# Two-layer diffusion backbone: attention maxima in other PSUM banks, five weight units in flight, later row sums, an output gate ahead of the heads

## The chip, the cores and the metric

The kernel runs on one core of one Trainium2 chip. The metric is the device time of one execution in microseconds (us), as the median of several runs. Everything below about durations and waits is read from one profiled execution of the kernel before the change.

## The reference, cut to what matters

Two layers work on 512 latent tokens (x) and 256 context tokens (ctx), 1024 channels, in float32. Each layer normalises, projects the tokens into three mixers, merges these by sigmoid gates, and ends with a gated MLP:

```python
for l in range(DEPTH):
    hx = rmsnorm(x, norm1_w[l]) * (1.0 + sc1) + sh1          # context likewise
    mix_x, mix_c = token_mixers(hx, hc, ...)
    x = x + g1 * mix_x
    x = x + g2 * conv_ffn(rmsnorm(x, norm2_w[l]) * (1.0 + sc2) + sh2, ...)
    # the context takes the same steps in layer 0 only
def token_mixers(hx, hc, ...):
    conv_x = conformer_conv(...)                             # depthwise, width 31
    h_x, h_c = mlstm_bidirectional(...)                      # 4 heads of 256, both directions
    mlstm_x = mlstm_readout(h_x, mo_x, ...)                  # rms norm, sigmoid(mo_x) as output gate
    attn_x = latent_attention(q_x, [k_c, k_x], [v_c, v_x])   # 8 heads of 64, 768 keys
    return (g_conv * conv_x + g_mlstm * mlstm_x + g_attn * attn_x) @ w_out
def attend(q, k, v):
    p = jax.nn.softmax(einsum(q, k) * 64 ** -0.5)            # each query's maximum is subtracted
```

## The kernel before, in words

Every float32 product is three products of rounded parts: a high part (`hh`, `B`, `AC`; `wh` for weights) and a low part (the remainder: `hl`, `C`; `wl`). A projection (`proj`, matmuls at L717) takes one 128x128 weight block at a time and multiplies it with the stretch of 512 latent and of 256 context columns into an `mm` tile in PSUM; a matmul over 512 columns issues every 0.23 us, one over 256 every 0.12 us.

**Weights.** A unit is four blocks (256 KB). Its DMA is queued on SP (`raw`), ScalarE (ACT) copies it to the high part `wh` (L215), and GpSimd (POOL) forms the low part `wl` (L217). The three tags have three buffers each, and units are split two ahead (`SPLITS`). In stretches with `shared` set, odd units are loaded into `P` tiles, and VectorE (DVE) forms their low part. These are the stretches in which matmuls have only 256 columns: the merge of the context in the first layer (1136 to 1165 us) and the start of its up projection, the context's part of the last down projection (1764 to 1790), and the second layer's merge (2597 to 2657) with the start of its up projection.

**PSUM.** Two `pv` tiles and two `sm` tiles of 512 columns; `mm` has two tiles of 1024 columns in the first layer and four of 512 in the second (`banks`). Projections use `mm`; `pv` takes the accumulator of the attention's value product (L1565), the maxima's scores (L1472, L1479) and the maxima's transposes (L1489).

**Order.** Each engine runs its instructions in the order in which the program is written; `Filler` sets that order. `step()` issues one piece of projection work on TensorE (PE), and `tick()` counts down the side chains (`chain`), which say with `yield n` after how many ticks their next piece is issued. Ticks set only the order: an instruction then waits for its inputs, and everything behind it on the same engine waits too.

**Gates.** `mgates` turns the mLSTM gate rows into decay terms: a chain of small DVE operations (L852 to L893) with two ACT operations between, and at its end four PE matmuls (`sm<-t,cst`, L904).

**mLSTM heads.** Tables `HEADS` and `HEADS1` (second layer) give, per head, the projections that fill it (`c` convolution taps, `o0 o1` output gates, `q`, `v` of the next head) and the tick of each step. `S` multiplies three pairs of scores, `score_gap` ticks apart, and sums them into `den` (DVE, L1131); `R` (`normalise`) sums `den` over rows by PE (L584), sends the result through a DMA and applies it (DVE, L1157); `V` multiplies with the values. Indices 0 and 1 are the two column groups.

**Attention.** `prepare(i)` needs, per head, each query's maximum before `weigh` can exponentiate: four maxima of 512 latent keys (`mx`), then two of twice 256 context keys (`mc`), one `pv` tile and one DVE reduction each, `prep` ticks apart; then `rp`, a transpose of the maxima (L1489, L1490). In the first layer a pair of context queries follows. While head i+1 is prepared, `weigh` and L1565 finish head i: reciprocal (L1571) and scaling out of `pv` (L1573).

Of the kernel before, what the change touches and what calls it, by code (L numbers as in the profile page):

```python
# [10 lines left out]
F32R = mybir.dt.float32r  # L11
# [6 lines left out]
D = 1024  # L18
# [32 lines left out]
HEADS = [["c o0 o1 q v", "0:D1 2:S0 6:R0 9:S1 18:D2 22:V0 24:R1 26:S2 41:R2 44:V1 60:V2 60:D*"]] * 3 +     [["c o0 o1 b b x0", "0:D1 2:S0 6:R0 9:S1 18:D2 24:R1 26:S2 28:V0 40:R2 44:V1 52:s 56:V2"]]  # L51
HEADS1 = [["c o0 o1 q v", "2:S0 4:D1 16:R0 22:S1 39:R1 40:V0 61:V1 61:D*"]] * 3 +     [["c o0 o1 b b x0", "2:S0 4:D1 15:R0 21:S1 35:R1 38:V0 51:V1 51:s"]]
COMMON = dict(
    
    gates=[(branch, m) for branch in (1, 0, 2) for m in range(KC)],
    score_gap=5, rows_gap=4, mask_gap=2, prep=2)
OPT = [dict(COMMON, partial=2, heads=HEADS, early=1, first_max=5, send_gap=2, norm_gap=8, first="G v",
            fgroups=[4, 4, 4, 4, 2, 4], skew=2,
            exp2=(0, 1, 2, 3, 4, 5), lo_pool=(0, 1, 2, 5),
            ylo="p", add="d", dve_lo=(0, 2, 4, 6)),  # L60
       dict(COMMON, partial=3, heads=HEADS1, early=1, first_max=8, send_gap=3, norm_gap=11, first="Q g K v",
            fgroups=[4, 3, 4, 4, 3, 4], skew=1,
# [125 lines left out]
class Weights:  # L188


    def __init__(self, nc, dram, l, pool, more):
        self.next, self.shared, self.more = None, False, more
# [14 lines left out]
    def split(self, upto):  # L207
        if self.next and upto > self.units:
            self.next.split(upto - self.units)
        for u in range(len(self.parts), min(upto, self.units)):  # L210
            self.load(u + 1)
            raw = self.raws.pop(u)
            hi = self.pool.tile([128, UNIT * 128], F32R, tag="wh", name=f"wh{self.l}_{u}")
            lo = self.pool.tile([128, UNIT * 128], F32R, tag="wl", name=f"wl{self.l}_{u}")
            self.nc.scalar.activation(out=hi, in_=raw, func=AF.Copy)  # L215
            eng = self.nc.vector if self.shared and u % 2 else self.nc.gpsimd
            eng.tensor_tensor(out=lo, in0=raw, in1=hi.bitcast(F32), op=ALU.subtract)  # L217
            self.parts[u] = hi, lo

    def take(self, *specs):  # L220

        u, j = divmod(len(self.blocks), UNIT)
        if j == 0:
            self.split(u + 1)
        if j <= 1 < j + len(specs):
            self.split(u + SPLITS + 1)
        if j + len(specs) == UNIT:
            self.load(u + LOADS + 1 + 3 * self.shared)
        self.blocks += specs
        o = slice(j * 128, (j + len(specs)) * 128)  # L230
        return [part[:, o] for part in self.parts[u]]
# [56 lines left out]
def build(tc, A):  # L288
# [3 lines left out]
    with ExitStack() as es:  # L292
# [462 lines left out]
        more = lambda u: alloc("P", PB, UNIT * 128)  # L755
        W = Weights(nc, A["ws"], 0, wp, more)
        first = ada_first()
# [19 lines left out]
        for l in range(DEPTH):  # L777
# [10 lines left out]
            if wc:  # L788
                W.next = Weights(nc, A["ws"], l + 1, wp, more)
            plans.append(W.blocks)  # L790
# [35 lines left out]
            def mgates(gp):  # L826
# [16 lines left out]
                for P_, nat, sc in dirs:  # L843
# [12 lines left out]
                yield 1  # L856
                act.activation(out=ln[R, :], in_=u[R, :], func=AF.Ln)
                act.activation(out=u[R, :], in_=ln[R, :], func=AF.Exp, scale=-1.0)
                dve.tensor_tensor(out=e[R, :], in0=e[R, :], in1=u[R, :], op=ALU.mult)
                yield 2  # L860
                dve.tensor_tensor(out=ln[R, :], in0=ln[R, :], in1=e[R, :], op=ALU.subtract)
                yield 1
# [3 lines left out]
                yield 2  # L866
                dve.tensor_tensor_scan(out=ms[R, :], data0=lf[R, :], data1=li[R, :], initial=NEG, op0=ALU.add, op1=ALU.max)
                yield 2
                dve.tensor_tensor_scan(out=g[R, :], data0=rm[R, :], data1=lf[R, :], initial=0.0, op0=ALU.mult, op1=ALU.add)
                yield 2  # L870
                rr, em, be = z, e, u
                for P_, nat, sc in dirs:
                    dve.tensor_tensor(out=rr[P_, nat], in0=g[P_, sc], in1=ms[P_, sc], op=ALU.subtract)
                act.dma_start(out=rdram, in_=rr[R, :])
                yield 1
                for P_, nat, sc in dirs:
# [4 lines left out]
                for d in range(1, NB):  # L881
# [3 lines left out]
                    else:  # L885
# [4 lines left out]
                                  in1=selrow[R].rearrange("p (n o) -> p n o", o=1).to_broadcast([36, 8, 15]), op=ALU.mult)  # L890
                yield 3
# [3 lines left out]
                yield 2  # L895

# [408 lines left out]
            for what in opt["first"].split():  # L1305
# [147 lines left out]
            def prepare(i):  # L1453
# [13 lines left out]
                for o, n, s in own:  # L1467
                    q0, nb = o // 128, n // 128
                    if s == 0:
                        for qb in range(q0, q0 + nb):  # L1470
                            ps = pv()
                            pe.matmul(ps, q1[:, qb * 128:qb * 128 + 128], ks_[v_][:, 0:L], start=True, stop=True)  # L1472
                            dve.reduce_max(out=mx[:, qb:qb + 1], in_=ps, axis=AX.X)
                            yield opt["prep"]
                    m_ = mc if s == 0 else mx
                    for qb in range(q0, q0 + nb, 2):
                        ps = pv()
                        for j in range(2):
                            pe.matmul(ps[:, j * C:j * C + C], q1[:, (qb + j) * 128:(qb + j) * 128 + 128], ks_[v_][:, L:T],  # L1479
                                      start=(j == 0), stop=True, skip_group_check=True)  # L1480
                        dve.reduce_max(out=m_[:, qb:qb + 2], in_=ps.rearrange("p (j n) -> p j n", j=2), axis=AX.X)
                        if qb + 2 < q0 + nb:
                            yield opt["prep"]
                    if s == 0:
# [286 lines left out]
```

## Time and profile before

| | |
|---|---|
| median of 3 runs | 3040.97 us (3040.7 to 3048.51) |
| profiled execution, own time | 3040.4 us |
| its span in the trace | 3038.6 us |
| mean granted TensorE clock | 0.973 of full speed |
| PE busy | 2827.8 us, 93% of the span |
| DVE, ACT, POOL busy | 60%, 38%, 38% |

The span lies 1.8 us below the execution's own time. Idle time counts only on an engine that others wait for; here that is PE.

### The profile page before, as it was taken

Reading aid. Unit: us, or ns where it says so; the run is one execution under the profiler, and the core shown is the slowest. Engines: PE = TensorE matmul, PEld = TensorE weight load, DVE = VectorE, ACT = ScalarE, POOL = GpSimd, SP = SyncE. Lnnn points to the kernel's source line nnn. Section 1 sums busy time; section 2 is a strip of 40 time slices with the busy share of each in tenths; the row PEclk is TensorE's granted clock in tenths of the full one; section 3 lists DMA queues with packets and bytes.
Section 4 is the critical chain, followed back from the end, with each engine's and each line's share of the span. In section 5 each row is a group of like instructions: output and inputs, shape, how many; then the busy total and the mean of one; then the engine's idle time right before and its main releaser. Section 6 shows DMA issues by size and latency. Waiting matters only on the chain. (4 is left out here: it accounts for less than half of the span.)

```text
span 3038.6 us, 42068 instructions
## 1 busy us (share of the span) xinstructions
PE 2827.8 (93%) x15970; PEld 2381.7 (78%) x15970; DVE 1817.7 (60%) x2521; ACT 1156.8 (38%) x2122; POOL 1146.6 (38%) x931
## 2 busy tenths in 40 slices
PE   7999999899889998999999988999889889899999
PEld 4888888787667887888888867887767567778887
DVE  4376787825554336876765555777774763554444
ACT  5224334324345334322322253433444344443333
POOL 2233343224244334333333333333344345444444
PEclk9999999999999999999999999999999999999999
DMA  6454334221010242333333232333322112423333
GB/s 242 133 149 69 58 67 68 49 60 52 28 28 29 63 130 93 115 101 118 118 115 115 75 102 68 65 75 67 65 75 69 39 38 76 154 87 100 93 96 110
DMA packets 156681, 262.47 MB, mean 86 GB/s; under 512 B 17784, under 2 KB 37624, under 8 KB 156480
## 3 DMA queue, kind: packets, MB, share of 16 engines
q1 hardware_dynamic: 142560, 249.67, 28.0%
q10 hardware_dynamic: 13920, 10.12, 3.1%
q8 instruction: 126, 2.06, 0.3%
q14 instruction: 75, 0.61, 0.1%
HBM read 247.05 MB, written 5.46 MB: 83 GB/s over the span
## 5 line engine op out<-in xcount | busy, mean ns | idle before, releaser
L217 POOL TENSOR_TENSOR wl<-raw,wh 128x512 fp32r<-128x512 f32 x659 | 904.6, 1379 | 1507.6 <-ACT wh L215 1461.0
L717 PE MATMUL mm<-hh,wh 128*128 128x512 f32 (+1 forms) x2672 | 963.6, 361 | 17.0 <-DVE big L1619 7.1
L717 PE MATMUL mm<-hh,wl 128*128 128x512 f32 (+1 forms) x2672 | 949.1, 355 | 10.7 <-POOL wl L217 10.6
L717 PE MATMUL mm<-hl,wh 128*128 128x512 f32 (+1 forms) x2672 | 954.4, 357 | 2.1 <-POOL hl L372 1.2
L215 ACT ACTIVATE wh<-raw 128x512 fp32r<-128x512 f32 x662 | 411.2, 625 | 580.2 <-PE mm L717 358.4
L717 PEld LDWEIGHTS mm<-hh,wh 128*128 128x128 f32 x2672 | 512.4, 192 | 113.3 <-issue 29.6
L717 PEld LDWEIGHTS mm<-hh,wl 128*128 128x128 f32 x2672 | 510.4, 191 | 89.4 <-POOL wl L217 15.5
L717 PEld LDWEIGHTS mm<-hl,wh 128*128 128x128 f32 x2672 | 512.3, 192 | 71.4 <-POOL hl L372 1.8
L717 PE MATMUL mm<-C,wh 128*128 128x512 f32 (+1 forms) x1168 | 410.2, 351 | 0.3 <-DVE C L372 0.3
L717 PE MATMUL mm<-B,wh 128*128 128x512 f32 (+1 forms) x976 | 344.4, 353 | 24.4 <-DVE big L1619 11.8
L717 PE MATMUL mm<-B,wl 128*128 128x512 f32 (+1 forms) x976 | 342.5, 351 | 9.2 <-POOL wl L217 8.8
L993 DVE SCALAR_TENSOR_TENSOR AC<-G,par,AC 128x783 f32<-128x783 f32 (+1 forms) x240 | 261.1, 1088 | 3.6
L717 PEld LDWEIGHTS mm<-C,wh 128*128 128x128 f32 x1168 | 226.6, 194 | 28.3 <-DVE C L372 0.5
L717 PEld LDWEIGHTS mm<-B,wh 128*128 128x128 f32 x976 | 190.1, 195 | 53.7 <-ACT wh L215 14.5
L717 PEld LDWEIGHTS mm<-B,wl 128*128 128x128 f32 x976 | 189.4, 194 | 37.4 <-POOL wl L217 14.2
L1669 DVE SCALAR_TENSOR_TENSOR AC<-mm,par,AC 128x511 f32<-128x511 f32 (+1 forms) x132 | 86.7, 656 | 199.0 <-ACT AC L1667 199.0
L1619 DVE SCALAR_TENSOR_TENSOR big<-mm,mod,big 128x512 f32<-128x512 f32 (+1 forms) x144 | 91.1, 657 | 116.3 <-PE mm L717 116.1
L1667 ACT ACTIVATE AC<-mm,par 128x768 f32<-128x768 f32 (+1 forms) x88 | 77.4, 880 | 145.0 <-PE mm L717 144.8
L372 POOL TENSOR_TENSOR P<-t,P 128x512 fp32r<-128x512 f32 (+1 forms) x64 | 75.1, 1175 | 139.2 <-ACT t L1550 111.2
L527 DVE SCALAR_TENSOR_TENSOR P<-C,cs,P 128x512 f32<-128x512 f32 x112 | 116.5, 1072 | 0.9 <-DMA C<-aw 0.9
L1565 PE MATMUL pv<-P,B 128*128 128x512 f32 (+1 forms) x336 | 94.6, 387 | 12.1 <-DVE G L1573 5.2
L1097 ACT ACTIVATE C<-rb,bias 128x128 f32<-128x128 f32 x312 | 96.4, 390 | 21.4 <-DMA rb<-rows 11.2
(282 smaller groups left out, 3726.5 us busy)
## 6 DMA issues: line engine op xcount, KB each, us to landing
raw<-ws SPq DMA_DIRECT2D x662, 256.0 KB, 2.6
C<-aw SPq DMA_DIRECT2D x104, 256.0 KB, 3.0
big<-aw SPq DMA_DIRECT2D x64, 256.0 KB, 4.7
P<-ws SPq DMA_DIRECT2D x30, 256.0 KB, 2.9
big<-xt SPq DMA_DIRECT2D x16, 384.0 KB, 6.3
rb<-rows ACTq DMA_DIRECT2D x40, 128.0 KB, 4.2
den<-rd ACTq DMA_DIRECT2D x40, 64.0 KB, 6.3
den<-rd SPq DMA_DIRECT2D x40, 64.0 KB, 6.3
```

Of the source, the lines that this page charges most:

```text
L215: self.nc.scalar.activation(out=hi, in_=raw, func=AF.Copy)
L217: eng.tensor_tensor(out=lo, in0=raw, in1=hi.bitcast(F32), op=ALU.subtract)
L372: (eng or dve).tensor_tensor(out=out, in0=src, in1=hi.bitcast(F32), op=ALU.subtract)
L527: dve.scalar_tensor_tensor(out=a_, in0=r_, scalar=cs[:, k, q:q + 1], in1=a_, op0=ALU.mult, op1=ALU.add)
L717: pe.matmul(ps[:, o:o + n], w[w_], h[h_][:, so:so + n], start=(k == 0 and i == 0 and o % 512 == 0), stop=(k == n_k - 1 and i == 2), skip_g ...
L993: dve.scalar_tensor_tensor(out=a, in0=t[:, j:j + cw], scalar=par(l, "cw", w0 + j), in1=a, op0=ALU.mult, op1=ALU.add)
L1097: act.activation(out=t[:, off + x * 128:off + x * 128 + 128], in_=rb[:, c0:c0 + 128], func=AF.Exp, bias=bcol(dr, h, key, qb))
L1565: pe.matmul(o_[:, 0:n_q], vblock(b, a_)[:, 64 * v_:64 * v_ + 128], b_[:, 0:n_q], start=(ki == 0 and x == 0), stop=(last and x == 2))
L1619: dve.scalar_tensor_tensor(out=xs[m][:, o:o + n], in0=ps[:, po:po + n], scalar=gain[:, m, s:s + 1], in1=xs[m][:, o:o + n], op0=ALU.mult, o ...
L1667: act.activation(out=t[:, 0:tq], in_=ps[:, 0:tq], func=AF.Identity, scale=fw(1), bias=fb)
L1669: dve.scalar_tensor_tensor(out=t[:, o + 1:o + n], in0=ps[:, o:o + n - 1], scalar=fw(0), in1=t[:, o + 1:o + n], op0=ALU.mult, op1=ALU.add)
```

## The change

Four edits. (A) The maxima over the head's own keys are written to `mm` tiles, as many query blocks to a tile as fit (`banks[1] // L`): in the first layer two latent maxima of 1024 columns and one context maximum of 1024 for a head; in the second layer the counts stay and only the bank changes. The context's own queries stay in `pv`. (B) In `shared` stretches odd units put both parts into the four `AC` tiles (`room`), so that five units can be split instead of three, and splits run one unit further ahead. (C) In the second layer `score_gap` is 4 instead of 5, the first row sums stand at tick 18 instead of 16 and the second at 41 instead of 39 in heads 0 to 2, with the second scores at 25 instead of 22; head 0 loses `o0`. (D) `mgates` yields 33 ticks instead of 21 in all, in both layers, and the second layer issues the first output gate (`o`) before `v`.

```diff
-HEADS1 = [["c o0 o1 q v", "2:S0 4:D1 16:R0 22:S1 39:R1 40:V0 61:V1 61:D*"]] * 3 + ...
+HEADS1 = [["c o1 q v", "2:S0 4:D1 18:R0 25:S1 41:R1 42:V0 60:V1 60:D*"]] + [["c o0 o1 q v", "2:S0 4:D1 18:R0 25:S1 41:R1 42:V0 61:V1 61:D*"]] * 2 + ...
-       dict(COMMON, partial=3, heads=HEADS1, early=1, first_max=8, send_gap=3, norm_gap=11, first="Q g K v",
+       dict(COMMON, partial=3, score_gap=4, heads=HEADS1, early=1, first_max=8, send_gap=3, norm_gap=11, first="Q g K o v",
...
-            hi = self.pool.tile([128, UNIT * 128], F32R, tag="wh", name=f"wh{self.l}_{u}")
-            lo = self.pool.tile([128, UNIT * 128], F32R, tag="wl", name=f"wl{self.l}_{u}")
+            if self.shared and u % 2:
+                hi, lo = self.room(), self.room()
+            else:
+                hi = self.pool.tile([128, UNIT * 128], F32R, tag="wh", name=f"wh{self.l}_{u}")
+                lo = self.pool.tile([128, UNIT * 128], F32R, tag="wl", name=f"wl{self.l}_{u}")
...
-            self.split(u + SPLITS + 1)
+            self.split(u + SPLITS + 1 + self.shared)
...
+        room = lambda: tac(UNIT * 128, F32R)
...
-                yield 5
+                yield 6
                 dve.tensor_scalar(out=u[R, :], in0=e[R, :], scalar1=1.0, scalar2=None, op0=ALU.add)
...
+                elif what == "o":
+                    fill.add(o_gate(0, 0))
...
+                    for to, keys_, per in ((mx, slice(0, L), banks[1] // L), (mc, slice(L, T), banks[1] // C)):
+                        if s:
+                            to, per = mx, 2
+                        if s and keys_.start == 0:
+                            continue
+                        nk = keys_.stop - keys_.start
+                        for qb in range(q0, q0 + nb, per):
+                            ps = mm(per * nk) if s == 0 else pv()
+                            for j in range(per):
+                                pe.matmul(ps[:, j * nk:j * nk + nk], q1[:, (qb + j) * 128:(qb + j) * 128 + 128],
+                                          ks_[v_][:, keys_], start=(j * nk % 512 == 0), stop=True, skip_group_check=True)
+                            dve.reduce_max(out=to[:, qb:qb + per], in_=ps[:, 0:per * nk].rearrange("p (j n) -> p j n", j=per),
+                                           axis=AX.X)
+                            if keys_.start == 0 or qb + per < q0 + nb:
+                                yield opt["prep"]
```

What this moves on DVE is seen in one head of the first layer's attention. Before, from the last two latent maxima on:

```order
L1473 TENSOR_REDUCE mx_7898<-pv_7989 128x1
L1481 TENSOR_REDUCE mc_7899<-pv_8004 128x2
L1481 TENSOR_REDUCE mc_7899<-pv_8017 128x2
L1485 TENSOR_TENSOR mx_7898<-mx_7898,mc_7899 128x4
L369 SCALAR_TENSOR_TENSOR t_807_8039<-sig_7952,mm_7972 128x768
L1446 TENSOR_TENSOR big_6097<-big_6097,t_807_8039 128x768
L1571 RECIPROCAL den_8045<-den_8045 128x256
L1573 TENSOR_TENSOR G_7002<-pv_7910,den_8045 64x256 x2
L1490 SCALAR_TENSOR_TENSOR C_7893<-pv_8051,cst 4x512
L1481 TENSOR_REDUCE mx_7898<-pv_8070 128x2
L1490 SCALAR_TENSOR_TENSOR C_7893<-pv_8097,cst 2x256
```

In the changed kernel, from the second maximum on (line numbers are some nine higher; the maxima over own keys now come from `mm`):

```order
L1489 TENSOR_REDUCE mx_7874<-mm_7931 128x2
L376 TENSOR_TENSOR P_7942<-t_781_7944,P_7941 128x512
L1489 TENSOR_REDUCE mc_7875<-mm_7947 128x4
L1494 TENSOR_TENSOR mx_7874<-mx_7874,mc_7875 128x4
L1499 SCALAR_TENSOR_TENSOR C_7869<-pv_7974,cst 4x512
L1489 TENSOR_REDUCE mx_7874<-pv_7992 128x2
L373 SCALAR_TENSOR_TENSOR t_794_8016<-sig_7929,mm_7954 128x768
L1454 TENSOR_TENSOR big_6097<-big_6097,t_794_8016 128x768
L1499 SCALAR_TENSOR_TENSOR C_7869<-pv_8019,cst 2x256
L1580 RECIPROCAL den_8025<-den_8025 128x256
L1582 TENSOR_TENSOR G_7004<-pv_7886,den_8025 64x256 x2
```

The reciprocal and the scaling of the head before (`RECIPROCAL`, `G`) stood ahead of the transposed maxima (`C`) and of the context's maximum (`128x2`); now these stand ahead of the reciprocal.

On PE the maxima now take the `mm` tile that the open projection leaves free. One place of the changed kernel in the first layer; `mm_7675` is the projection that has just begun, `mm_7682` and `mm_7698` are maxima:

```order
L721 MATMUL mm_7675<-AC_6852,wl_134_7531 128x256
L1487 MATMUL mm_7682<-B_6845,C_7638 128x512 x2
L1574 MATMUL pv_7652<-P_7632,B_6796 128x512
L1574 MATMUL pv_7652<-P_7633,B_6796 128x512
L1574 MATMUL pv_7652<-P_7632,B_6797 128x512
L1553 MATMUL sm_7689<-C_7053,B_6845 128x512
L1554 MATMUL sm_7689<-C_7054,B_6847 128x512
L1487 MATMUL mm_7698<-B_6845,C_7638 128x512 x2
L721 MATMUL mm_7675<-AC_6928,wh_134_7530 128x512
L721 MATMUL mm_7675<-C_6929,wh_134_7530 128x512
```

The tile of `mm_7682` is that of the projection that ended just before `mm_7675`, and `mm_7698` takes the tile of `mm_7682`; before, both were in `pv`.

On DVE the gate chain of the second layer stood nearly in one piece before (`L372` is a low part of a key projection):

```order
L861 TENSOR_TENSOR C_16188<-C_16188,C_16186 36x768
L372 TENSOR_TENSOR B_16273<-mm_16204,B_16272 128x512
L372 TENSOR_TENSOR B_16273<-mm_16205,B_16272 128x256
L864 SCALAR_TENSOR_TENSOR C_16189<-C_16185,C_16188 32x512
L864 SCALAR_TENSOR_TENSOR C_16189<-C_16185,C_16188 32x256
L864 SCALAR_TENSOR_TENSOR C_16189<-C_16185,C_16188 4x512
L864 SCALAR_TENSOR_TENSOR C_16189<-C_16185,C_16188 4x256
L867 SCALAR_TENSOR_TENSOR C_16190<-C_16189,C_16184 36x768
L869 SCALAR_TENSOR_TENSOR C_16191<-sig_16200,C_16189 36x768
```

In the changed kernel the low parts of both key projections stand within it:

```order
L376 TENSOR_TENSOR B_16224<-mm_16156,B_16223 128x512
L376 TENSOR_TENSOR B_16224<-mm_16157,B_16223 128x256
L866 TENSOR_TENSOR C_16140<-C_16140,C_16138 36x768
L869 SCALAR_TENSOR_TENSOR C_16141<-C_16137,C_16140 32x512
L869 SCALAR_TENSOR_TENSOR C_16141<-C_16137,C_16140 32x256
L869 SCALAR_TENSOR_TENSOR C_16141<-C_16137,C_16140 4x512
L869 SCALAR_TENSOR_TENSOR C_16141<-C_16137,C_16140 4x256
L872 SCALAR_TENSOR_TENSOR C_16142<-C_16141,C_16136 36x768
L376 TENSOR_TENSOR B_16298<-mm_16229,B_16297 128x512
L376 TENSOR_TENSOR B_16298<-mm_16230,B_16297 128x256
L874 SCALAR_TENSOR_TENSOR C_16143<-sig_16152,C_16141 36x768
```

The chain's operations are the same; one projection's low part (two operations) that came after it now stands ahead of its second scan (`C<-sig,C`).

## Rows read from the trace of the kernel before

**Rows 1.** The page, part 1: busy us, share of the span, instructions.

```profile
PE 2827.8 (93%) x15970; PEld 2381.7 (78%) x15970; DVE 1817.7 (60%) x2521; ACT 1156.8 (38%) x2122; POOL 1146.6 (38%) x931
```

**Rows 2.** Waits of PE, whole span: total us, times, longest us.

```profile
PE sm L584 <- DVE den L1131: 31.8, 13, 4.0
PE pv L1472 <- DVE mx L1473: 24.0, 19, 6.6
PE mm L717 <- POOL wl L217: 20.2, 27, 2.6
...
PE sm L904 <- DVE t L889: 11.7, 2, 8.6
```

**Rows 3.** Eight half-clock stretches: one window (PEclk behind POOL), and the sum, busy us.

```profile
2061.60:2068.40 6.80, 5.99 (x20) 4.23 (x21) 5.88 (x10) 0.00 (x0) 0.25 (x1) 0.50 0.22 42
...
sum 30.70, PE 29.89 PEld 25.30 DVE 23.07 ACT 6.95 POOL 6.34; mean PE 3.74 PEld 3.16 DVE 2.88 ACT 0.87 POOL 0.79
```

**Rows 4.** Waits of PE, first-layer attention: 740 to 815, then 815 to 960.

```profile
PE pv L1472 <- DVE mx L1473: 7.1, 3, 6.6
...
PE pv L1565 <- DVE G L1573: 4.4, 2, 2.2
PE pv L1479 <- DVE G L1573: 4.2, 2, 2.3
PE pv L1565 <- DVE B L1573: 2.2, 1, 2.2
...
PE pv L1479 <- DVE B L1573: 1.9, 1, 1.9
```

**Rows 5.** Groups on DVE 735 to 1000, and one on ACT 815 to 960.

```profile
L1473 DVE TENSOR_REDUCE mx<-pv 128x1 f32<-128x512 f32 x32 | 21.8, 685 | 8.5 <-PE pv L1472 8.4
...
L1047 DVE TENSOR_TENSOR t<-G,rb 32x512 f32<-32x512 f32 x4 | 6.2, 1555 | 0.1
...
L1573 DVE TENSOR_TENSOR G<-pv,den 64x256 f32<-64x256 f32 x8 | 3.4, 422 | 0.5
...
L1573 DVE TENSOR_TENSOR G<-pv,den 64x128 f32<-64x128 f32 x8 | 2.3, 289 | 0.5
...
L1018 ACT ACTIVATE sig<-mm,par 128x768 f32<-128x768 f32 x5 | 4.5, 904 | 0.6 <-PE mm L717 0.6
```

**Rows 6.** Waits of PE, second-layer attention: 2345 to 2375, then 2375 to 2512.

```profile
PE pv L1472 <- DVE mx L1473: 5.3, 1, 5.3
...
PE pv L1472 <- DVE mx L1473: 9.4, 11, 2.0
```

**Rows 7.** Merges: waits, splits (ns min/median/max), a window (PE, PEld, DVE, ACT, POOL busy).

```profile
PE mm L717 <- POOL wl L217: 3.6, 4, 1.3
PE mm L717 <- ACT wh L215: 3.3, 3, 1.3
...
PE mm L717 <- POOL wl L217: 4.2, 9, 0.9
PE mm L717 <- ACT wh L215: 4.1, 4, 2.3
...
L217 DVE TENSOR_TENSOR wl<-P,wh x13: 683/1347/1397, 2608.5 to 2653.5; 128x512 fp32r<-128x512 f32 x13
...
1136.00:1165.00 29.00, 22.11 (x142) 20.50 (x141) 22.31 (x35) 13.65 (x24) 9.63 (x8) 0.86 0.37 115
```

**Rows 8.** Residual of the last down projection: waits of PE, 1764 to 1790.

```profile
PE mm L717 <- DVE big L1619: 14.3, 4, 7.1
```

**Rows 9.** PE at row sums of the second layer, timeline: start, us, wait.

```profile
1872.09 0.92 PE L584 MATMUL sm<-den,cst 128*32 128x128 f32 x8 [0.70 <-DVE den L1131]
...
1896.74 0.92 PE L584 MATMUL sm<-den,cst 128*32 128x128 f32 x8 [3.48 <-DVE den L1131]
...
1967.24 0.92 PE L584 MATMUL sm<-den,cst 128*32 128x128 f32 x8 [3.11 <-DVE den L1131]
```

**Rows 10.** The end of the second layer’s gate chain on DVE.

```profile
1835.38 0.27 DVE L889 TENSOR_TENSOR t<-t,cst 36x120 f32<-36x120 f32 x1
```

More of the change, by code (lines that the diff above doesn't have):

```diff
@@ L51 @@
 HEADS = [["c o0 o1 q v", "0:D1 2:S0 6:R0 9:S1 18:D2 22:V0 24:R1 26:S2 41:R2 44:V1 60:V2 60:D*"]] * 3 +     [["c o0 o1 b b x0", "0:D1 2:S0 6:R0 9:S1 18:D2 24:R1 26:S2 28:V0 40:R2 44:V1 52:s 56:V2"]]
-HEADS1 = [["c o0 o1 q v", "2:S0 4:D1 16:R0 22:S1 39:R1 40:V0 61:V1 61:D*"]] * 3 +     [["c o0 o1 b b x0", "2:S0 4:D1 15:R0 21:S1 35:R1 38:V0 51:V1 51:s"]]
+HEADS1 = [["c o1 q v", "2:S0 4:D1 18:R0 25:S1 41:R1 42:V0 60:V1 60:D*"]] + [["c o0 o1 q v", "2:S0 4:D1 18:R0 25:S1 41:R1 42:V0 61:V1 61:D*"]] * 2 +     [["c o0 o1 b b x0", "2:S0 4:D1 15:R0 21:S1 35:R1 38:V0 51:V1 51:s"]]
 COMMON = dict(
     gates=[(branch, m) for branch in (1, 0, 2) for m in range(KC)],
-    score_gap=5, rows_gap=4, mask_gap=2, prep=2)
-OPT = [dict(COMMON, partial=2, heads=HEADS, early=1, first_max=5, send_gap=2, norm_gap=8, first="G v",
+    rows_gap=4, mask_gap=2, prep=2)
+OPT = [dict(COMMON, partial=2, score_gap=5, heads=HEADS, early=1, first_max=5, send_gap=2, norm_gap=8, first="G v",
             fgroups=[4, 4, 4, 4, 2, 4], skew=2,
@@ L188, with __init__ @@
 class Weights:
-    def __init__(self, nc, dram, l, pool, more):
-        self.next, self.shared, self.more = None, False, more
+    def __init__(self, nc, dram, l, pool, more, room):
+        self.next, self.shared, self.more, self.room = None, False, more, room
         self.nc, self.dram, self.l, self.pool = nc, dram, l, pool
@@ L755, in build @@
         more = lambda u: alloc("P", PB, UNIT * 128)
-        W = Weights(nc, A["ws"], 0, wp, more)
+        room = lambda: tac(UNIT * 128, F32R)
+        W = Weights(nc, A["ws"], 0, wp, more, room)
         first = ada_first()
@@ L788, in build @@
             if wc:
-                W.next = Weights(nc, A["ws"], l + 1, wp, more)
+                W.next = Weights(nc, A["ws"], l + 1, wp, more, room)
             plans.append(W.blocks)
@@ L855, in mgates @@
                                          op1=ALU.subtract)
-                yield 1
+                yield 2
                 act.activation(out=ln[R, :], in_=u[R, :], func=AF.Ln)
@@ L859, in mgates @@
                 dve.tensor_tensor(out=e[R, :], in0=e[R, :], in1=u[R, :], op=ALU.mult)
+                yield 3
+                dve.tensor_tensor(out=ln[R, :], in0=ln[R, :], in1=e[R, :], op=ALU.subtract)
                 yield 2
-                dve.tensor_tensor(out=ln[R, :], in0=ln[R, :], in1=e[R, :], op=ALU.subtract)
-                yield 1
                 for P_, nat, sc in dirs:
@@ L865, in mgates @@
                                              op1=ALU.subtract)
-                yield 2
+                yield 3
                 dve.tensor_tensor_scan(out=ms[R, :], data0=lf[R, :], data1=li[R, :], initial=NEG, op0=ALU.add, op1=ALU.max)
-                yield 2
+                yield 3
                 dve.tensor_tensor_scan(out=g[R, :], data0=rm[R, :], data1=lf[R, :], initial=0.0, op0=ALU.mult, op1=ALU.add)
-                yield 2
+                yield 3
                 rr, em, be = z, e, u
@@ L873, in mgates @@
                     dve.tensor_tensor(out=rr[P_, nat], in0=g[P_, sc], in1=ms[P_, sc], op=ALU.subtract)
+                yield 2
                 act.dma_start(out=rdram, in_=rr[R, :])
-                yield 1
+                yield 2
                 for P_, nat, sc in dirs:
@@ L890, in mgates @@
                                   in1=selrow[R].rearrange("p (n o) -> p n o", o=1).to_broadcast([36, 8, 15]), op=ALU.mult)
-                yield 3
+                yield 4
                 for P_, nat, sc in dirs:
@@ L894, in mgates @@
                                       op1=ALU.mult)
-                yield 2
+                yield 3
                 for dr in range(2):
@@ L1468, in prepare @@
                     q0, nb = o // 128, n // 128
[L1469 to L1483, printed above, removed]
+                    for to, keys_, per in ((mx, slice(0, L), banks[1] // L), (mc, slice(L, T), banks[1] // C)):
[13 more added lines that the diff above has]
+                                yield opt["prep"]
                     if s == 0:
```

## Prediction

> **What bounds the kernel now.** I read the page's engine table first: PE is busy 2827.8 us, 93% of the span [rows 1], so 3038.6 - 2827.8 = 210.8 us of PE idleness is all that an edit that removes no matmul can win, besides time in which PE runs at half rate. Then the waits of PE [rows 2]: the reader is to see that no single wait dominates. Four of its rows are what the edits touch: row sums behind `den` (31.8 us), maxima behind an earlier reduction (24.0), low weight parts (20.2) and the gate chain (11.7). Last the windows around the longest waits. [...]
>
> **A, first layer.** In the steady part (815 to 960) the largest waits are four groups that end on the scaling L1573, 4.4 + 4.2 + 2.2 + 1.9 = 12.7 us in six waits of about 2.1 [rows 4]. Each time PE wants a `pv` tile while the accumulator of the head before holds one until DVE has done the reciprocal and the scaling. The order on DVE shows the new place: the maxima are finished ahead of that reciprocal, and what is late next, the next accumulator's tile, comes one short context item later. I count the 12.7 as gone. A reduction over 512 columns takes 0.685 us [rows 5]; one over 1024 is not in the trace. Bounds: 0.685 and twice that, 1.37. I take 1.22, from the slope of the scaling out of `pv`, 0.289 us for 128 columns and 0.422 for 256 [rows 5]: 0.289 + 7 x 0.133. DVE's own work thus falls a little (six 0.685 become three 1.22, -0.4 us a head).
>
> The price is in `mm`: two tiles, one held by the open projection. The second maximum waits for the first one's reduction. Between them PE issues about five 512-column matmuls, 1.2 us by 0.23 each, against 1.22 plus perhaps a `P` low part; that leaves 0.3 to 0.9 us. The first maximum, where a projection has just ended, waits for its evacuation, 0.904 us on ACT [rows 5], behind six matmuls worth 1.05: about 0.3. The third has about 1 us of cover against 1.22 again. I take 0.7 + 0.5 = 1.2 us for each of six heads, 7 us; bounds 0 (covered) and 3 x 1.2 x 6 = 22 (nothing covers). Of the waits in the first two heads, 7.1 us at L1472 [rows 4], nearly all is four rope operations that take 6.2 us of DVE [rows 5]. The maxima's reductions still stand behind the rope on DVE and the transpose L1498 comes soon on PE, so I keep 5 us of them and save 2, and 3 for the smaller waits behind the next rope steps. Term: -12.7 + 7 - 5 = -10.7, bounds -24 and +5.
>
> **A, second layer.** The order on PE and DVE is as before, only the tiles differ: four `mm` tiles of 512 of which a projection takes two, instead of two `pv` tiles of which the accumulator takes one. Waits at L1472 are 9.4 us in 11 after 2375, and 5.3 once behind the rope [rows 6]. The rope's wait stays, for the same reason as above; of the 9.4 I take 7 as gone, since two free tiles cover one reduction of 0.685. Bounds -14 (all) and 0 (the projection's evacuations hold the tiles instead). Term: -7.
>
> **B.** In the first merge the low parts cost PE 3.6 us and the high parts 3.3, in the second 4.2 and 4.1 [rows 7], 15.2 in all. They come in pairs: a high part stands behind norm work in ACT's order, so the low part starts late and PE waits twice. Splitting one unit earlier gives a unit's matmuls more lead: 12 matmuls of 0.12 us, 1.4 us, which is more than each single wait but the 2.3 one. But DVE is busy for 22.31 of the first merge's 29 us [rows 7], and the parts that come earlier take DVE's time from the norm chain. I take half, -7.5. Bounds -15.2 and 0. The last down projection waits 14.3 us on the residual L1619 [rows 8], a DVE chain; there the edit is worth nothing. The up projections' starts have a few such waits too; I count -1.
>
> A row that bears on this: a DVE split takes 0.683 us at the least and 1.347 in the median [rows 7], with POOL's split of the other unit running beside it. [...]
>
> **C.** Row sums in the second layer wait 0.70 us for the first head and 3.11 for the second [rows 9]; the third and fourth are like the second. The last pair's scores come 2 x 1 ticks earlier and the sums 2 later, so four more ticks, some 2.8 us of PE filler at three 512-column matmuls (0.7 us) a tick, lie between `den` and its use. That takes about 2.6 each from heads 1 and 2, 0.7 from head 0, and about 1 from head 3, whose table keeps its tick: -6.9. The second sums, 3.48 us at 1896.74 [rows 9] and three more like it, stay: they stand behind the first sums' DMA and the apply, and both moved by two ticks. Against it: head 0 loses a gate's eight ticks of filler, so convolution taps are left for head 1, about 3 us of DVE work there, of which I count 2 as a PE wait. Term: -4.9, bounds -10 and +3.
>
> **D.** In the second layer the chain ends on DVE at 1835.65 [rows 10], and PE has waited 8.6 us for it, from 1827 [rows 2, 10]. With `o_gate(0, 0)` ahead PE comes some 5.6 us later (8 blocks of three 512-column matmuls, 0.7 us each), at 1832.5. The order shows the second low part, 1 us, now within the chain, and two ACT splits ahead of its logarithm (0.6 us each): it ends at 1837 to 1839. The wait becomes 4.5 to 6.5, a saving of 3 on average; bounds -5.6 and +3. Behind L904 on PE stand only `v_proj` and the decay rows. In the first layer the wait is 11.7 - 8.6 = 3.1 us [rows 2]; the longer chain there falls behind a query's low part and nothing is put ahead of it, so I add 1.5, bounds 0 and +4. Term: -1.5.
>
> [...]
>
> **Sum.** -10.7 - 7 - 8.5 - 4.9 - 1.5 - 5 = -37.6 us, against the profiled execution's 3040.4: 3002.8. That execution is 0.6 below the median, so the forecast is 3003.
>
> **Rivals.**
> *Slower: the two `mm` tiles starve PE in the first layer.* A maximum that waits in `pv` delays attention; one that waits in `mm` stops the projection that is PE's filler, because the next projection needs the tile. There are 3 groups x 8 heads. If each waits a reduction and a `P` low part that stand unlucky on DVE, 1.22 + 0.7 = 1.9 us, that is 46 us instead of the 7 counted: 3003 + 39 = 3042; with new half-rate stretches as long as those seen, 3.4 us at half for every second head and more, 10 us, 3052. It decides from (38 + 7) / 24 = 1.9 us a group. For it: the rope's operations and low parts stand between reductions on DVE. Against: DVE sat idle 8.5 us ahead of the L1473 group, waiting for PE [rows 5], so its queue was often empty there.
>
> *The waits only move.* In the merges, the mLSTM heads and the gate chain DVE is what is late, and PE waits for it elsewhere: B gives 2, C 2, D 0, the clock 0, A 6 and 3. The sum is -13: 3028. For it: DVE's 22.31 us in the merge, the second row sums' unchanged 3.5 us each. Against: the six waits of rows 4 end on an order, not on DVE's load.
>
> *All of it.* The removed waits go with their half clock and no new ones come: A -12.7 - 7 - 14, B -15.2, C -9, D -5, clock -12: -75, 2966. Against: the rope and the DVE load.
>
> **Chances.** Forecast 0.60, only moved 0.20, all of it 0.12, starved 0.08. The likeliest case's own range is 2985 to 3020. The range that holds the time 8 times in 10 goes from 2975, short of the full recovery, to 3031, past the moved one. A measurement of this kernel tells about 0.3%, 9 us, from no change: below 3032 is faster, above 3050 slower. The forecast, full recovery and three quarters of the moved case are faster: 0.86; a quarter of the moved case and a third of the starved one are the same: 0.08; the rest, 0.06, is slower.
>
> **What would show it.** A: no wait of L1565 or of the context's maxima on L1582 in the first layer, and short ones of L1487 and L721 on the reductions L1489; in the second layer L1487 under 3 us after the rope. B: waits on low and high parts in the merges halved. C: L588 on `den` at the first sums under 1 us, at the second unchanged. D: L91x on its chain 5 to 6 us at the later place. I am wrong if L721 or L1487 wait over 1 us in most heads of the first layer, or if the windows behind the shortened waits still read 0.50.

## The result, and the profile after

The changed kernel takes 3000.08 us (median of 4 runs, 2995.7 to 3000.43) against 3044.74 (4 runs of the kernel before, 3040.7 to 3052.82): a ratio of 0.9847, 95% interval 0.9822 to 0.9872. 3003 was forecast. Later runs of the kernel before, 24 of them, had a median of 3044.64, so its profiled execution (3040.4) lies 4 us below its usual time, and the gain is some 45 us, not the 41 that the first median of 3040.97 gave.

The engine row of the page answers to [rows 1]:

```profile
PE 2811.4 (94%) x15970; PEld 2372.4 (79%) x15970; DVE 1813.5 (60%) x2497; ACT 1155.4 (39%) x2122; POOL 1151.3 (38%) x931
```

PE is idle for 2998.6 - 2811.4 = 187.2 us instead of 210.8, 23.6 less. Its busy time is 16.4 us less for the same 15970 matmuls: some 12 of these 16 us are matmuls that no longer run at half clock, for the stretches at a granted clock of 0.50 sum to 138 us instead of 163. Waits of PE over the whole span, as [rows 2]:

```profile
PE sm L588 <- DVE den L1137: 28.2, 13, 4.3
...
PE mm L721 <- POOL wl L221: 20.5, 25, 2.1
...
PE mm L1487 <- DVE mx L1489: 9.7, 12, 4.1
PE sm L910 <- DVE t L895: 9.3, 2, 5.4
...
PE pv L1498 <- DVE mx L1489: 5.8, 2, 5.1
```

The maxima fall from 24.0 to 9.7 us and the gate chain from 11.7 to 9.3. Of what the maxima lost, 5.8 us now stand at the transposes behind them (L1498), where the kernel before waited 2.9. The row sums still wait 28.2 us, 3.6 less than before, and the low parts 20.5, as before.

Both kernels issue the same 11520 weight matmuls (L717, L721). Laying the k-th of one trace over the k-th of the other tells where time was won; the table gives the change of each stage in us, negative where it is shorter (bounds by the times of the kernel before). The single parts are the experiments below; A+B is the kernel with these two parts.

```
stage, us of before             changed    A     B     C     D    A+B
0-592 gates, mLSTM heads, 1        +6.2  +3.1  +0.8  +2.3  +4.7  +0.5
592-988 attention, 1              -20.8 -20.9  -0.1  -0.1   0.0 -20.9
988-1208 merges, up start, 1       -3.7  +2.8  -4.6  +2.4  +2.2  -4.9
1208-1797 MLP, 1                   -4.2  -0.8  -1.2  -0.7  -0.6  -2.6
1797-2317 gates, heads, out, 2     +0.9  -2.2  +2.3  +1.3  -1.1  +0.3
2317-2516 attention, 2            -16.2 -16.2   0.0   0.0  -0.1 -16.1
2516-2708 merge, up start, 2       -2.2  +1.0  -2.4  -0.2  -0.7  -2.1
```

Two stages carry 37 of the 40 us by which the last of these matmuls is earlier. A second profile of the changed kernel (the last experiment) gives +2.7, -21.8, 0.0, -3.4, +1.7, -16.0 and -2.0 for the same lines: the two stages repeat within 1 us, others only within 4. Waits of PE in the first layer's attention, 740 to 820 and then 815 to 960 (their sums answer to [rows 4]):

```profile
PE pv L1498 <- DVE mx L1489: 5.1, 1, 5.1
PE mm L1487 <- DVE mx L1489: 2.4, 3, 1.4
...
PE mm L1487 <- DVE mx L1489: 2.5, 7, 0.5
PE mm L1487 <- ACT sig L1024: 0.9, 1, 0.9
PE pv L1498 <- DVE mx L1489: 0.7, 1, 0.7
```

No wait of this stage ends on the scaling (L1582) any more. The transposes' 5.1 us behind the rope stay. A reduction over 1024 columns, on DVE:

```profile
L1489 DVE TENSOR_REDUCE mx<-mm 128x2 f32<-128x1024 f32 x16 | 19.5, 1221 | 7.8 <-PE mm L1487 7.8
```

It takes 1.221 us; 1.22 had been taken from the slope. The granted clock of the first layer's attention, before and then after (it stands behind POOL's columns):

```profile
735.00:988.00 253.00, 222.69 (x1187) 177.77 (x1186) 144.63 (x202) 120.65 (x226) 101.52 (x86) 0.96 0.11 31
```

```profile
735.00:973.00 238.00, 222.20 (x1223) 180.01 (x1222) 148.96 (x182) 125.44 (x235) 107.41 (x91) 0.98 0.12 34
```

In the second layer's attention (2315 to 2480) the waits on reductions of own maxima are 4.8 us, of which 4.1 once behind the rope, against 5.3 + 9.4 [rows 6]:

```profile
PE mm L1487 <- DVE mx L1489: 4.8, 2, 4.1
PE pv L1498 <- DVE mx L1494: 3.2, 5, 1.0
```

### The profile page after: what moved, and what is told of

It reads as the page before. It is cut to its first block, busy times and chain, and to the rows that moved or that the text cites. A ratio compares the mean times of both kernels' runs of the same rounds, so it can differ in the third digit from the quotient of the medians.

```text
span 2998.6 us, 41995 instructions
## 1 busy us (share of the span) xinstructions
PE 2811.4 (94%) x15970; PEld 2372.4 (79%) x15970; DVE 1813.5 (60%) x2497; ACT 1155.4 (39%) x2122; POOL 1151.3 (38%) x931
## 3 DMA queue, kind: packets, MB, share of 16 engines
q8 instruction: 126, 2.06, 0.3%
## 5 line engine op out<-in xcount | busy, mean ns | idle before, releaser
L721 PE MATMUL mm<-hh,wh 128*128 128x512 f32 (+1 forms) x2664 | 960.9, 361 | 22.1 <-DVE big L1628 8.3
L721 PE MATMUL mm<-hh,wl 128*128 128x512 f32 (+1 forms) x2664 | 946.5, 355 | 15.1 <-POOL wl L221 15.0
L721 PE MATMUL mm<-hl,wh 128*128 128x512 f32 (+1 forms) x2664 | 951.5, 357 | 2.1 <-POOL hl L376 1.2
L721 PEld LDWEIGHTS mm<-hh,wh 128*128 128x128 f32 x2664 | 510.9, 192 | 120.5 <-issue 28.8
L721 PEld LDWEIGHTS mm<-hh,wl 128*128 128x128 f32 x2664 | 509.1, 191 | 94.8 <-POOL wl L221 21.7
L721 PEld LDWEIGHTS mm<-hl,wh 128*128 128x128 f32 x2664 | 510.9, 192 | 70.9 <-POOL hl L376 1.8
L721 PE MATMUL mm<-C,wh 128*128 128x512 f32 (+1 forms) x1068 | 377.1, 353 | 0.3 <-DVE C L376 0.3
L721 PE MATMUL mm<-B,wh 128*128 128x512 f32 (+1 forms) x876 | 311.2, 355 | 16.9 <-DVE big L1628 10.8
L721 PE MATMUL mm<-B,wl 128*128 128x512 f32 (+1 forms) x876 | 308.4, 352 | 4.8 <-POOL wl L221 4.7
L721 PEld LDWEIGHTS mm<-C,wh 128*128 128x128 f32 x1068 | 202.9, 190 | 28.2 <-DVE C L376 0.5
L721 PEld LDWEIGHTS mm<-B,wh 128*128 128x128 f32 x876 | 166.7, 190 | 44.7 <-issue 8.4
L721 PEld LDWEIGHTS mm<-B,wl 128*128 128x128 f32 x876 | 166.6, 190 | 30.4 <-POOL wl L221 8.0
L1628 DVE SCALAR_TENSOR_TENSOR big<-mm,mod,big 128x512 f32<-128x512 f32 (+1 forms) x144 | 91.0, 656 | 114.1 <-PE mm L721 114.0
L1188 PE MATMUL pv<-P,C 128*128 128x256 f32 x624 | 95.3, 290 | 5.8 <-DVE P L376 3.1
```

Of the source, the lines that this page charges most:

```text
L721: pe.matmul(ps[:, o:o + n], w[w_], h[h_][:, so:so + n], start=(k == 0 and i == 0 and o % 512 == 0), stop=(k == n_k - 1 and i == 2), skip_g ...
L1188: pe.matmul(ps[:, dd * 256:dd * 256 + 256], v_[key // 3][:, vo:vo + 128], b_, start=(ki == 0 and i == 0 and dd == 0), stop=(ki == len(part ...
L1628: dve.scalar_tensor_tensor(out=xs[m][:, o:o + n], in0=ps[:, po:po + n], scalar=gain[:, m, s:s + 1], in1=xs[m][:, o:o + n], op0=ALU.mult, o ...
```

## The experiments

**Each part alone.** Part A is the whole `prepare` hunk of the diff, part B the hunks of `Weights` and `room`; a line or two of each stand here.

A, the kernel before with only:

```diff
+                            ps = mm(per * nk) if s == 0 else pv()
```

B, the kernel before with only:

```diff
+            if self.shared and u % 2:
+                hi, lo = self.room(), self.room()
...
+            self.split(u + SPLITS + 1 + self.shared)
```

> The kernel before with part A alone (maxima in the projections' tiles). Theory: A carries nearly all of the gain, as the two traces say when they are laid over each other matmul by matmul (21 us in the first layer's attention, 16 in the second's): 3003 to 3008 us. Rival: the gain was shared as the prediction's terms say, 17.7 us of waits and some clock: 3017 to 3023 us.

> The kernel before with part B alone (five weight units in flight in shared stretches). Theory: about 6 us in the two merges and nothing in the up projections, since DVE's norm chain and the serial splits set the end there: 3033 to 3036 us. Rival: B also gives the 3 us that the first layer's MLP gained, since units are split earlier there: 3029 to 3032 us.

A alone: 3007.27 us, ratio 0.9875 (0.9859 to 0.9892), 38 us. B alone: 3034.39 us, ratio 0.9964 (0.9951 to 0.9977), 11 us, and in its trace -4.6 and -2.4 in the merges. Both are as the theory said. A carries most of the gain, and its two stages show the same -21 and -16 us as in the changed kernel.

C, the kernel before with only the later sums in heads 0 to 2 and the closer scores:

```diff
-"2:S0 4:D1 16:R0 22:S1 39:R1 40:V0 61:V1 61:D*"
+"2:S0 4:D1 18:R0 25:S1 41:R1 42:V0 61:V1 61:D*"
-score_gap=5
+score_gap=4
```

D, the kernel before with the longer yields and the gate ahead of head 0 (whose last steps stand at 60):

```diff
-first="Q g K v"
+first="Q g K o v"
-["c o0 o1 q v", "2:S0 4:D1 16:R0 22:S1 39:R1 40:V0 61:V1 61:D*"]
+["c o1 q v", "2:S0 4:D1 16:R0 22:S1 39:R1 40:V0 60:V1 60:D*"]
...
-                yield 5
+                yield 6
```

> The kernel before with part C alone (later row sums in the second layer; head 0 keeps its first output gate). Theory: the wait at the first sums falls by 5 to 6 us, but the pieces of the apply that move with it stand ahead of weight splits on POOL and ACT, so that 4 to 6 us of waits for low weight parts come before the second sums: no change, within 3 us of 3041. Rival: these waits come from the gate moved in part D; then C alone is 5 us faster: 3035 to 3037 us.

> The kernel before with part D alone (longer yields in the gate chain of both layers, an output gate ahead of the second layer's heads; row sums as before). Theory: 3 us less wait and 3 us less half clock in the second layer, and the 5 us that the first layer's heads lost come from half-clock stretches that fall differently from execution to execution, so 3035 to 3040 us and first-layer heads as before. Rival: the longer chain in the first layer is what costs those 5 us: 3040 to 3045 us, with the loss between 105 and 600 us in its trace.

C alone: 3045.91 us, ratio 1.0004 (0.9995 to 1.0013). D alone: 3045.36, ratio 1.0001 (0.999 to 1.0011). Neither moves the time by more than 0.13%. For C this is as expected, and its trace has the waits for low weight parts that were expected, 4.2 us in the second layer's heads. For D a gain of some 3 us of wait and 3 of half clock was expected, and the time shows neither this nor the loss that the rival had. In D's trace, on PE (start, us, wait), the gate chain's wait is 5.40 us, as the changed kernel's 5.41, instead of 8.6:

```profile
1844.11 0.78 PE L905 MATMUL sm<-t,cst 36*128 36x120 f32 x2 [5.40 <-DVE t L890]
...
1957.33 0.42 PE L584 MATMUL sm<-t,cst 128*32 128x128 f32 x8 [2.04 <-DVE t L1193]
...
1971.87 0.38 PE L584 MATMUL sm<-den,cst 128*32 128x128 f32 x2 [2.69 <-DVE den L1132]
1973.32 0.42 PE L584 MATMUL sm<-den,cst 128*32 128x128 f32 x6 [1.07 <-DVE den L1132]
```

At that place D has won some 3.5 us, its gate's matmuls counted as work done. The rows behind it show where they go: at the start of the next head, the head norm's sums and the first row sums wait 2.04, 2.69 and 1.07 us, where the kernel before waited 3.11 in all [rows 9]. Head 0 has lost its gate's matmuls, and some 5 us are given back by 2100; the wait of 2.04 us stands in all six profiles whose head 0 lacks the gate, and in none of the other eight.

**A and B without C and D.**

The tables, the yields and the first projections are those of the kernel before; of the diff there are only

```diff
+            self.split(u + SPLITS + 1 + self.shared)
...
+                            ps = mm(per * nk) if s == 0 else pv()
```

> Parts A and B without C and D. Theory: C and D are worth nothing together, as each was alone: 2997 to 3003 us, the same as the changed kernel. Rival: they pay only together (head 0 lost its gate's ticks, which later sums make up for): 3004 to 3010 us.

2996.76 us, ratio 0.985 (0.9833 to 0.9866): the same as the changed kernel within the intervals. C and D are worth nothing here that these runs can tell, alone or together.

**What in A brings the first layer's gain: the place in the order, or the tile?**

First the kernel before with its maxima in `pv` but closer together in the first layer:

```diff
-prep=2
+prep=1
```

> The kernel before, with the maxima still in pv tiles but one tick apart instead of two in the first layer, so that a head's preparation ends about as early as in the changed kernel. Theory (the place in the order brings the first layer's gain): the waits on the scaling go, 12.7 us, but with one free pv tile each maximum waits for the reduction ahead of it, some 0.3 us in 36 cases: 3036 to 3042 us. Rival (the tiles alone bring it): the waits on the scaling stay and the new ones come on top: 3050 to 3060 us.

Then the changed kernel with maxima as narrow as before, in `mm`:

```diff
-for to, keys_, per in ((mx, slice(0, L), banks[1] // L), (mc, slice(L, T), banks[1] // C)):
+for to, keys_, per in ((mx, slice(0, L), 1), (mc, slice(L, T), 2)):
```

> The changed kernel with one query block of 512 latent keys and two of 256 context keys to a maximum, as before, but in the mm tiles: six mm tiles a head in the first layer instead of three; the second layer is unchanged. Theory (order): preparation ends as late as before, so the waits of the context's maxima and of the next accumulator on the scaling return, 10 to 13 us: 3010 to 3014 us. Rival (tiles): own maxima out of pv are enough: 2999 to 3003 us. Second rival: six takes of the spare tile starve the projections, 0.5 us each: 3024 us and more.

With an earlier end but still in `pv`: 3040.66 us, ratio 0.9993 (0.9984 to 1.0003), and the attention 2.8 us shorter. Its waits of PE from 812 to 955:

```profile
PE pv L1472 <- DVE mx L1473: 5.5, 10, 0.9
PE pv L1479 <- DVE mc L1481: 3.2, 6, 0.8
PE pv L1565 <- DVE G L1573: 2.1, 2, 1.2
```

The scaling costs 2.1 us here, and 0.9 in another row, instead of the 12.7 of [rows 4], but the maxima now wait for one another, 5.5 us in ten and 3.2 in six. In `mm`, but as six narrow maxima: 3028.55 us, ratio 0.9952 (0.9937 to 0.9966), some 28 us slower than the changed kernel. Its waits in the same stretch, and the clock of its attention (735 to 1004):

```profile
PE pv L1574 <- DVE G L1582: 4.4, 2, 2.2
PE pv L1487 <- DVE G L1582: 4.2, 2, 2.3
PE mm L1487 <- DVE mx L1489: 2.9, 7, 0.7
PE pv L1487 <- DVE B L1582: 1.9, 1, 1.9
...
735.00:1004.00 269.00, 234.84 (x1223) 186.87 (x1222) 146.71 (x205) 125.37 (x235) 105.19 (x89) 0.95 0.10 31
```

The waits on the scaling are back to the tenth, 4.4 + 4.2 + 1.9 and 2.2 behind 955, although no own maximum is in `pv`. Preparation ends late again, and the context's maxima and the accumulators still need `pv`. The stage is 31 us longer than in the changed kernel: its waits (all rows from 735 on) are 34.0 us instead of 15.7, of which the scaling is 12.7 and waits in `mm` are 17.3 instead of 8.8, and 27.3 us at half clock instead of 10.2 cost another 8.5. The time lies in the second rival's range, but the greater part of the added waits is the theory's. So neither the earlier place alone nor the other tile alone does it: three wide maxima, which bring both, end the preparation early without crowding either pool. Whether the width itself is needed is open: narrow maxima in `mm` one tick apart, which bring both too, were not run.

**The apply in C.** The changed kernel waits for low weight parts just ahead of second row sums, which the kernel before did not (PE: start, us, wait):

```profile
1873.92 0.50 PE L721 MATMUL mm<-hh,wl 128*128 128x512 f32 x1 [2.00 <-POOL wl L221]
...
1877.96 1.15 PE L588 MATMUL sm<-den,cst 128*32 128x128 f32 x8 [3.18 <-DVE den L1137]
...
1945.19 0.42 PE L588 MATMUL sm<-den,cst 128*32 128x128 f32 x6 [0.96 <-DVE den L1137]
...
1972.91 1.15 PE L588 MATMUL sm<-den,cst 128*32 128x128 f32 x8 [3.54 <-DVE den L1137]
```

The changed kernel with the apply earlier in the second layer:

```diff
-norm_gap=11
+norm_gap=9
```

> The changed kernel with norm_gap 9 instead of 11 in the second layer, so that the apply stands at the same ticks of a head as before the change although the row sums stand two later. Theory: the low weight parts ahead of the second sums are late because the apply's pieces moved ahead of them on POOL and ACT; they come in time again and 4 to 6 us are gained: 2994 to 2997 us. Rival: the apply then waits for the row sums' DMA and holds DVE, so that the second sums come later instead: 3000 to 3006 us.

And parts A and B with, of C, only this in the second layer:

```diff
-score_gap=5
+score_gap=4
```

> Parts A and B, and of C only score_gap 4 in the second layer: the last pair's scores come two ticks earlier, the row sums and the apply stay where they were before. Theory: each first row sum waits 1.4 us less and no piece of the apply moves ahead of a split, so 4 to 6 us less than A and B alone: ratio 0.983 to 0.9835 to the kernel before, 2991 to 2994 us where A and B gave 2996.8. Rival: DVE's sums are no earlier, because DVE is busy with convolution taps: as A and B alone.

With the apply two ticks earlier: 3005.96 us, ratio 0.9874 (0.986 to 0.9889), slower than the changed kernel; the rival held. The wait for the low part is 0.35 us instead of 2.00, but DVE now waits 2.06 us for the sums' DMA ahead of the apply, and the second sums' wait grows to 6.51:

```profile
1880.76 1.15 PE L588 MATMUL sm<-den,cst 128*32 128x128 f32 x8 [6.51 <-DVE den L1137]
```

With closer scores alone: 2996.2 us, ratio 0.9835 (0.9821 to 0.9848), the same as A and B. The forecast gain did not come. Head 1's first and second sums in its trace:

```profile
1939.84 0.92 PE L588 MATMUL sm<-den,cst 128*32 128x128 f32 x8 [1.27 <-DVE den L1136]
...
1966.91 1.15 PE L588 MATMUL sm<-den,cst 128*32 128x128 f32 x8 [5.56 <-DVE den L1136]
```

The first sums wait 1.27 us instead of the 3.11 of the kernel before, the second 5.56 instead of 3.44. What one wait loses the other takes.

**What in B: more tiles, or an earlier split?**

The changed kernel with

```diff
-            self.split(u + SPLITS + 1 + self.shared)
+            self.split(u + SPLITS + 1)
```

> The changed kernel with tiles for five units, but splits no further ahead than before. Theory (lead): the merges' waits on high and low parts come back, since the tiles alone start no split earlier: 3006 to 3010 us, the loss all in the two merges and the up projections' starts. Rival (room): the splits had been held back by their tiles, and lead without them was worth little: 2999 to 3002 us.

3008.3 us, ratio 0.9878 (0.9864 to 0.9892), some 9 us slower than the changed kernel. In its trace both merges with the starts of the up projections are as long as before the change or longer, +2.2 and +1.0. Waits of PE in the first merge (1120 to 1160):

```profile
PE mm L721 <- POOL wl L221: 6.3, 5, 2.6
PE mm L721 <- ACT wh L219: 3.4, 3, 1.4
```

Of the 6.3 us one wait of 2.6 belongs to the up projection behind it; the rest, 3.7 and 3.4, is as [rows 7], 3.6 and 3.3. The tiles only make room; the gain comes with the lead. The lead without the tiles was not run.

The lead does a second thing, which no run separates from the first: it turns the order of the two splits around. In the kernel before, DVE's split starts while POOL's runs, and takes 1.35 us, where a lone one takes 0.63 to 0.69:

```profile
2617.59 1.30 POOL L217 TENSOR_TENSOR wl<-raw,wh 128x512 fp32r<-128x512 f32 x1 [2.35 <-ACT wh L215]
2618.09 1.35 DVE L217 TENSOR_TENSOR wl<-P,wh 128x512 fp32r<-128x512 f32 x1 [0.64 <-ACT wh L215]
```

In the changed kernel DVE's comes first. DVE's splits of the second merge (ns min/median/max), there and then without the lead, answer to [rows 7]:

```profile
L221 DVE TENSOR_TENSOR AC<-P,AC x14: 676/693/1223, 2570.4 to 2615.6; 128x512 fp32r<-128x512 f32 x14
L221 DVE TENSOR_TENSOR AC<-P,AC x15: 680/1350/1393, 2580.2 to 2635.7; 128x512 fp32r<-128x512 f32 x15
```

This frees 4 to 5 us of DVE in each merge.

**What in D: the yields or the gate?**

A and B, and of D the longer yields alone, of which the first is

```diff
-                yield 5
+                yield 6
```

> Parts A and B, and of D only the longer yields; the output gate stays in head 0. Theory: the chain ends later and PE comes as early as before, so the second layer's wait grows from 8.6 to 9.5 to 12 us and the first layer's by 1; 2 to 5 us slower than A and B alone: 2998 to 3002 us. Rival: it is the yields that saved 3 us in part D: 2993 to 2995 us.

2997.34 us, ratio 0.984 (0.9824 to 0.9856), not told apart from A and B, and outside both forecasts. The second layer's wait is 8.8 us and the first layer's 3.9, so the chain ended hardly later; the 3 us of wait that D saves come from the gate's matmuls ahead of it, not from the yields.

**The same kernel again.**

> The changed kernel once more, beside the others. Theory: the stretches at half clock lie elsewhere in this execution, above all in the first layer's heads, where the trace showed 20 us of them with no change of code; the time is within 4 us of 3000. Rival: they lie where they did, because the order of the code sets them: 3000 with the same stretches.

2998.86 us, ratio 0.9845 (0.9832 to 0.9859). The clock of the first layer's heads (105 to 600) in this execution, and then in the changed kernel's first profile:

```profile
105.00:600.00 495.00, 471.41 (x3219) 411.57 (x3220) 344.94 (x496) 182.32 (x410) 169.49 (x146) 0.99 0.40 81
```

```profile
105.00:600.00 495.00, 472.24 (x3201) 412.32 (x3202) 344.01 (x492) 183.03 (x411) 166.55 (x145) 0.97 0.39 80
```

The code is the same, and 0.99 stands against 0.97. A stretch that lies across 105 us is in both; behind it there are 10.2 us at half clock against 20.5. So the theory holds for this stage; elsewhere, above all behind the long waits, most stretches lie where they did, though not all for as long; their sum is 138 us both times.

## Why the prediction was right, point by point

The time lies within 3 us of the forecast, and part of that is luck. The sum started from 3040.4 us, 4 below the usual time of the kernel before: the forecast gain of 38 us fell short of the measured 45. And the terms were off in opposite directions: A brought some 20 us more than its two terms, most of the clock's term in it, C and D 6 less.

**A, first layer: mechanism right, size too small.** -10.7 us was forecast without clock; the stage gave -21. The waits of the stage fell from 30.0 to 15.8 us (all rows of the two windows), 14.2 less, and half clock accounts for about 5 more. The mis-sized step is the price in `mm`: 7 us was taken for the six heads of the steady part, and the rows show 2.5 on reductions and 0.9 on an evacuation. In the first two heads 5 us were to be saved, and the waits fell by 2.8 only. The 12.7 us on the scaling are gone, as predicted, and the rope's 5 us stay, as predicted. That the reductions would starve the projections did not come about: six narrow maxima, twice as many, waited for the tile only 2.9 + 0.8 us in the steady part.

**A, second layer: too small again.** -7 forecast, -16.2 measured. After the rope 0.7 us of the 9.4 on reductions are left, the rope's own wait fell from 5.3 to 4.1, and 2.6 us on context maxima, which the prediction did not count, went with them: 12.5 us, of which other waits took back 1 (all waits of the stage fell from 28.8 to 17.4). Half clock in the stage fell from 17.1 to 10.2 us, 3.4 more. That the step to four tiles would help this much, with the order unchanged, was counted too cautiously.

**B: the size right, the way in part.** -8.5 forecast; alone it measured 0.36%, 11 us, and by the traces 7 in the two merges. That the lead is what pays is shown by taking it away. How it pays is only in part what was forecast. Nothing was counted for DVE's splits, which the lead makes half as long, 0.69 us in the median of the second merge instead of the 1.347 of [rows 7]; most splits of that row started while POOL's ran and ended 0.55 us behind it (see the last section). A pair of splits in the second merge, from the first start to the second end, took 1.84 us in the median before and 1.85 in the changed kernel. Five units in flight thus split no faster in pairs, and B was worth its term all the same, not the second rival's 2 us. And part of the wait moved as feared: in the changed kernel's first merge and second merge (1112 to 1147, 2557 to 2619) PE waits for

```profile
PE mm L721 <- DVE big L1628: 3.5, 2, 2.8
PE mm L721 <- POOL wl L221: 1.4, 2, 0.8
PE mm L721 <- ACT AC L219: 0.8, 1, 0.8
...
PE mm L721 <- ACT AC L219: 3.1, 3, 2.5
PE mm L721 <- POOL wl L221: 2.6, 5, 0.8
```

the residual (L1628) 3.5 us, which had no such row in [rows 7]. The waits of the first merge thus fall by no more than 1.0 us, from 6.9 to 5.9, and those of the second, of which the high and low parts were to be halved, by less than half. The rest of what the traces show is clock in the first merge's stage, 10.2 us at half against 13.7, and it does not stand fast: in the second profile of the changed kernel it is 20.5, and the stage is as long as before.

**C: wrong.** -4.9 forecast, nothing measured. The failed step is "That takes about 2.6 each from heads 1 and 2". The first sums' wait did shrink, to 0.96 in head 1, but `den`, the DMA of the sums, the apply and the next `den` follow one another and end hardly earlier, if at all: from a head's first scores to the end of its second sums it was 40.1, 42.5, 44.3 and 41.8 us in the four heads, and is 41.0, 44.1, 45.7 and 41.2 with C alone. PE, having waited less at the first sums, waits behind them instead. In the changed kernel it does so for low weight parts: row sums cost 18.5 us in these heads instead of 23.6, and low parts 6.2, where the kernel before had no such wait. With the earlier apply, or with closer scores alone, it waits at the second sums. "The second sums stay" was the sentence that should have been drawn to its end: a chain whose end stays gives nothing. The closer scores alone show it best, 1.8 us off one wait and 2.1 onto the next. That is the second rival's mechanism, in this one stage.

**D: the wait right, the account wrong.** The second layer's wait fell by 3.2 us to 5.41, as forecast:

```profile
1815.16 0.78 PE L910 MATMUL sm<-t,cst 36*128 36x120 f32 x2 [5.41 <-DVE t L895]
```

But the gate's matmuls had been filler in head 0, where 2 us of loss were counted under C; 5 were lost. The first layer's chain cost 0.8 us of wait, 1.5 was taken.

**Clock: right in kind.** The -5 in the sum was the author's estimate, and no run shows it as a term of its own. What the traces show in its place: the granted clock reads 0.50 in stretches of 3.4 to 13.7 us in the kernel before, in which a matmul over 512 columns issues every 0.43 us instead of 0.23; they sum to 163 us there and to 138 in the changed kernel's trace, which is some 12 us of time. About 5 of it is the first layer's attention and 3 the second's. The rest moved with the waits or fell by chance (below).

Of the rivals, starvation is refuted for three wide maxima, "all of it" did not happen because the rope, the second sums and the residual stayed, and "the waits only move" holds for C and the merges' residual. The chance of faster that was given, 0.86, adds up to 0.87.

## What to carry to other kernels

Before moving a step of a chain that another engine paces, follow the chain to its next meeting with the busy engine: if that one's time does not change, a wait taken away at the first meeting comes back at the second. Where short-lived results share buffers with long-lived accumulators, count both how many takes the short ones need and when the last one falls; fewer, wider takes from the pool that turns over anyway served both here. And compare traces by the k-th instruction of the bound engine: it showed two stages with all the gain, and two edits with none, which the totals by wait did not.

## What the runs showed of the hardware

How much time PE spends at half clock in the same code differs from execution to execution. In the first layer's heads (from 112 to 600 us), which no edit but D's gate chain touches, fourteen profiles hold between 6.8 and 20.5 us at 0.50: 6.8 in the kernel before, 20.5 and 10.2 in two profiles of the changed one, 20.5 with A alone. Between them lie up to 7 us of time, which accounts for most of the +6.2 in the first line of the table, and for why single profiles cannot tell edits of 0.2%.

Where the splits' subtractions on DVE and on POOL, each with both inputs in SBUF, overlap in the traces, the one that started later ended a nearly fixed time behind the other, whenever it had started. In the trace of the kernel before, 18 of DVE's splits start while one subtraction of POOL runs, 0.28 to 1.18 us behind its start; they take from 0.73 to 1.55 us, and every one of them ends 546 to 550 ns behind POOL's end, where a lone split takes 0.63 to 0.69 us. In the changed kernel DVE's split starts first in 14 pairs, takes 0.68 to 0.69 us in 12 of them, and POOL's ends 1.15 to 1.22 us behind it.
